# Attention: the first head pair's softmax factors are turned once and read back as rows

## The chip, the core and the metric

The kernel runs on one core of a Trainium2 chip. TensorE multiplies matrices from SBUF into PSUM (eight banks of 128 x 512 float32), VectorE, ScalarE and GpSimd work elementwise, SyncE issues most DMA transfers between DRAM and SBUF. Each engine executes its own instructions in order, and waits at an instruction until what it needs is there. GpSimd works on SBUF alone here: everything that it reads or writes is an SBUF tile. The metric is the device time of one execution in microseconds (us); of the kernel before it is 1876.85 us, the median of three runs (1876.06 to 1878.15).

## The reference, cut to what matters

The program is one decoder layer for 1024 tokens of width 1024 in float32: a half-step feed-forward network, then two token mixers side by side (attention and pooling), merged by gates, then another half-step feed-forward network. Only the attention is touched. It has three groups of four heads of 64 dimensions, each group with its own window and dilation, and the groups' results are combined per head with weights from their softmax denominators:

```python
for g, (window, dilation) in enumerate(DILATED_GROUPS):
    o, lse = dilated_window_attention(q[:, :, hs], k[:, :, hs], v[:, :, hs], window, dilation)
    outs.append(o)
    lses.append(lse)
alpha = jax.nn.softmax(jnp.stack(lses, axis=0), axis=0)
o = jnp.sum(alpha[..., None] * jnp.stack(outs, axis=0), axis=0)
return o.reshape(B, S, ATTN_OUT_WIDTH).astype(v.dtype)
```

So for each token and head there are three factors, one per group. The kernel folds the division by the denominator into them.

## The kernel before, in words

Every float32 product is done as three products of parts (a rounded high part and the low remainder), so most operands exist as a "hi" tile that ScalarE rounds and a "lo" tile that VectorE or GpSimd subtracts.

The attention is one loop over q from 0 to 23. The four heads of a group make two head pairs (hp 0 and 1); a slot s is one block of 128 queries of one head pair and group, for both heads, and there are N = 48 of them, 24 for each pair, in the order of groups 0, 1, 2 for the first pair and 1, 2, 0 for the second. Step q does the work of slots 2q and 2q+1, spread over three steps:

- `scores` (L1948, every second q for two steps ahead): TensorE multiplies queries by keys into PSUM banks with the tag "mm", of which there are four.
- `masked` (L1966, VectorE) adds the mask and keeps the row minimum; `exponents` (L1975, ScalarE) follows and leaves the row sums. Minimum and sum are a slot's statistics.
- one step later `trans_p` (L1995, TensorE) transposes the weights into banks of the tag "acc", four as well; `split_p` makes hi (L2007, ScalarE) and lo (L2010, VectorE).
- two steps later `values` (L2028, TensorE) multiplies by the values into an "acc" bank, and a step after that `gather` (L2051, VectorE) copies the result to the tile `own[hp, g]`: 128 partitions, 64 dimensions of the one head and 64 of the other, by 1024 tokens.

Between these TensorE fills in chunks of four matmuls of the pooling branch (`branch`, L2087, tiles yp), whose banks (also "acc") VectorE empties in `end_branches` (L2101). For ring tiles of the next group, ScalarE and GpSimd split queries and keys (`split_ring`, L1587 and L1588), and in slots 16 to 34 they prepare weights (`first_w_o`, L1823 to L1827).

The statistics of a group go through DRAM to be put in token order (`send_stats`, `get_stats`). From them `make_factors` makes a tile f of 128 tokens x 3 groups x 8 blocks x 2 heads for a head pair. It is a generator that `house` moves on one step at a time: for the first pair at slots 32, 33 and 34, with GpSimd doing most of the arithmetic, and for the second after the loop, with VectorE. It ends by spreading each factor over 64 places (`f_of`), for the first pair on GpSimd (L1913).

`combine(hp, half, ...)` is another generator. For each half of the tokens and each group it turns four blocks of the spread factors with TensorE (`factor_rows`, L1926), which puts them into an "mm" bank with the head dimension along the partitions, as `own` has it; VectorE multiplies `own` by them (L2060), GpSimd adds the groups (L2062), then ScalarE rounds (L2067) and GpSimd subtracts (L2068). For the first pair it is moved on two steps at a time in the odd steps q = 19, 21 and 23 and finished after the loop; there the second pair follows. Both results go into `merge` (L2153) after that.

The order on every engine is the order in which the program calls these functions (`tc.manual_schedule()`). All DMAs named here are issued by SyncE and stand in its order too.

Of the kernel before, what the change touches and what calls it, by code (L numbers as in the profile page):

```python
# [16 lines left out]
P = 128  # L17
# [120 lines left out]
def tile_block(  # L138
# [1748 lines left out]

    f_of = {}

    def make_factors(hp, eng):  # L1890
        st = stats[hp]
        m, l = st[:, :, :, 0:2], st[:, :, :, 2:4]
        top = att_small.tile([P, 1, NT, 2], F32, name=f"top{hp}")
        w = att_small.tile([P, GROUPS, NT, 2], F32, name=f"w{hp}")
        f = att_small.tile([P, GROUPS, NT, 2], F32, name=f"f{hp}")
        every = [P, GROUPS, NT, 2]
        ve.tensor_tensor(top[:, 0], m[:, 0], m[:, 1], op=OP.min)
        ve.tensor_tensor(top[:, 0], top[:, 0], m[:, 2], op=OP.min)
        eng.tensor_tensor(w, top.to_broadcast(every), m, op=OP.subtract)
        yield  # L1900
        ac.activation(w, w, AF.Exp)
        yield
        eng.tensor_tensor(f, w, l, op=OP.mult)
        eng.tensor_tensor(top[:, 0], f[:, 0], f[:, 1], op=OP.add)
        eng.tensor_tensor(top[:, 0], top[:, 0], f[:, 2], op=OP.add)
        ve.reciprocal(top, top)
        eng.tensor_tensor(f, w, top.to_broadcast(every), op=OP.mult)

        f_of[hp] = sums_o.tile([P, GROUPS, NT * 2, HD], F32, tag="f", bufs=1, name=f"f_of{hp}")
        for g in range(GROUPS):  # L1910
            src = f[:, g].rearrange("p i a -> p (i a)")[:, :, None].to_broadcast([P, NT * 2, HD])
            if hp == 0:
                gp.tensor_copy(f_of[hp][:, g], src)  # L1913
            elif g == 1:
                ve.tensor_copy(f_of[hp][:, g], src)
            else:
                ac.activation(f_of[hp][:, g], src, AF.Copy)
        yield
# [136 lines left out]
    def combine(hp, half, adds, lower):  # L2055
# [3 lines left out]
        for g in range(GROUPS):  # L2059
            ve.tensor_tensor(o[g], o[g], factor_rows(hp, g, half), op=OP.mult)  # L2060
            if g > 0:
# [105 lines left out]
    def house(s):  # L2167
# [6 lines left out]
        if u > 0 and i == 4 and slots[s - 5][1] != 0:  # L2174
            get_stats(*slots[s - 5][:2])
        if N // 2 + 8 <= s < N // 2 + 11:
            advance(factors[0])
# [6 lines left out]
    with tc.manual_schedule():  # L2184
# [8 lines left out]
        for q in range(N // 2):  # L2193
            send()
            if q % 2 == 0:
                scores(q)
                scores(q + 1)
            elif N // 4 + 7 <= q:
                advance(combines[0][(q - N // 4 - 7) // 4], 2)
            if q == 0 or q % 2 == 1:  # L2200
# [464 lines left out]
```

## Time and profile before

| | before |
|---|---|
| median of three runs | 1876.85 us |
| profiled execution | 1876.94 us, its span 1874.9 us |
| granted TensorE clock | 0.999 |
| busy: TensorE, VectorE, ScalarE, GpSimd | 99%, 73%, 41%, 42% |
| first pair's transposes of factors (L1926) | from 1098.9 us, 24 of the 48 |
| first pair's GpSimd spreads (L1913) | three, from 1096.1 us |

The span is the time from the first to the last instruction that the profile shows. Busy shares are over the whole span. Matmuls overlap one another, so a busy TensorE need not be at its peak: the distance between the starts of matmuls tells more than their lengths. Names such as L1926 are lines of the program. Of a waiting instruction the profile names the engine whose result came last.

### The profile page before, as it was taken

Reading aid. Unit: us, or ns where it says so; the run is one execution under the profiler, and the core shown is the slowest. Engines: PE = TensorE matmul, PEld = TensorE weight load, DVE = VectorE, ACT = ScalarE, POOL = GpSimd, SP = SyncE. Lnnn points to the kernel's source line nnn. Section 1 sums busy time; section 2 is a strip of 40 time slices with the busy share of each in tenths; the row PEclk is TensorE's granted clock in tenths of the full one; section 3 lists DMA queues with packets and bytes.
Section 4 is the critical chain, followed back from the end, with each engine's and each line's share of the span. In section 5 each row is a group of like instructions: output and inputs, shape, how many; then the busy total and the mean of one; then the engine's idle time right before and its main releaser. Section 6 shows DMA issues by size and latency. Waiting matters only on the chain.

```text
span 1874.9 us, 24458 instructions
## 1 busy us (share of the span) xinstructions
PE 1864.6 (99%) x8690; PEld 1546.4 (82%) x8690; DVE 1369.0 (73%) x1972; ACT 767.7 (41%) x1392; POOL 782.5 (42%) x566
## 2 busy tenths in 40 slices
PE   9999999999999999999999999999999999999998
PEld 7888888888888888888888888888888888888887
DVE  7887866668886776658885896888765566577867
ACT  8322323333345643334445762463333333334344
POOL 4554644452222364445554457544333333313221
PEclk9999999999999999999999999999999999999999
DMA  8134324356565435765678868734342233354654
GB/s 327 45 124 148 122 95 151 123 200 210 189 234 197 158 114 204 253 221 185 213 251 327 309 223 296 266 133 180 119 140 85 90 107 121 127 200 158 224 198 146
DMA packets 147473, 338.10 MB, mean 180 GB/s; under 512 B 17944, under 2 KB 39448, under 8 KB 145816
## 3 DMA queue, kind: packets, MB, share of 16 engines
q1 hardware_dynamic: 143608, 325.70, 50.3%
q10 hardware_dynamic: 3744, 10.85, 1.5%
q8 instruction: 68, 1.11, 0.3%
q14 instruction: 53, 0.43, 0.1%
HBM read 235.90 MB, written 100.60 MB: 179 GB/s over the span
## 4 chain that ended last, share of the span: by engine, by line
PE 54%; DVE 3%; ACT 2%; issue 1%; DMA 1%; POOL 1%; ACTq 0%; SPq 0%; DVEq 0%; POOLq 0%
PE u_mixm L334 15%; PE d_f L904 8%; PE wo L2345 4%; PE yp L2087 1%; PE u_f20a L334 1%; PE u_f21b L334 1%; PE u_f20b L334 1%; PE u_f21a L334 1%; PE u_f210b L334 1%; PE u_f210a L334 1%; PE u_f29b L334 1%; PE u_f29a L334 1%; PE u_f28b L334 1%; PE u_f28a L334 1%; PE u_f27b L334 1%
## 5 line engine op out<-in xcount | busy, mean ns | idle before, releaser
L904 PE MATMUL d_f<-bhi_f,ahi_f 128*128 128x512 f32 x616 | 240.2, 390 | 0.0
L904 PE MATMUL d_f<-bhi_f,alo_f 128*128 128x512 f32 x616 | 239.8, 389 | 0.0
L904 PE MATMUL d_f<-blo_f,ahi_f 128*128 128x512 f32 x616 | 239.6, 389 | 0.0
L861 POOL TENSOR_TENSOR alo_f<-g_f,ahi_f 128x512 fp32r<-128x512 f32 x60 | 89.6, 1511 | 266.2 <-ACT ahi_f L857 266.2
L334 PE MATMUL u_mixm<-xhi_t_mix,wc_mixm 128*128 128x512 f32 x608 | 157.3, 391 | 0.1
L904 PEld LDWEIGHTS d_f<-bhi_f,alo_f 128*128 128x128 f32 x616 | 115.6, 188 | 24.5 <-DVE alo_f L861 0.2
L904 PEld LDWEIGHTS d_f<-bhi_f,ahi_f 128*128 128x128 f32 x616 | 115.7, 188 | 24.2 <-ACT h L424 0.5
L904 PEld LDWEIGHTS d_f<-blo_f,ahi_f 128*128 128x128 f32 x616 | 115.7, 188 | 23.7
L334 PEld LDWEIGHTS u_mixm<-xhi_t_mix,wc_mixm 128*128 128x128 f32 x608 | 113.5, 188 | 23.8 <-ACT wc_mixm L322 0.6
L334 PE MATMUL u_mixm<-xhi_b_mix,wc_mixm 128*128 128x512 f32 x456 | 120.3, 391 | 0.0
L325 POOL TENSOR_TENSOR wc_mixm<-s_mixm,wc_mixm 128x512 fp32r<-128x512 f32 x52 | 77.9, 1499 | 99.1 <-ACT wc_mixm L322 88.2
L334 PEld LDWEIGHTS u_mixm<-xhi_b_mix,wc_mixm 128*128 128x128 f32 x456 | 85.0, 188 | 17.2
L322 ACT ACTIVATE wc_mixm<-s_mixm 128x512 fp32r<-128x512 f32 x76 | 47.0, 628 | 110.4 <-DVE s_mixm L378 54.1
L857 ACT ACTIVATE ahi_f<-g_f 128x1024 fp32r<-128x1024 f32 x84 | 81.9, 975 | 7.9 <-DMA g_f<-gs_f 7.9
L334 PE MATMUL u_mixm<-xlo_t_mix,wc_mixm 128*128 128x512 f32 x304 | 81.3, 389 | 0.0
L325 POOL TENSOR_TENSOR wc_mixm<-raw,wc_mixm 128x512 fp32r<-128x512 f32 x41 | 62.3, 1524 | 38.7 <-ACT wc_mixm L322 35.2
L2345 PE MATMUL wo<-w_o,o_hi 128*128 128x512 f32 x224 | 69.3, 390 | 0.0
L646 POOL TENSOR_TENSOR y_f<-y_f,norm_ffn 128x512 f32<-128x512 f32 x35 | 54.4, 1560 | 35.5 <-DVE y_f L627 25.2
L857 ACT ACTIVATE bhi_f<-s_f2w 128x512 fp32r<-128x512 f32 x55 | 32.9, 628 | 86.2 <-DVE s_f2w L879 67.3
L857 ACT ACTIVATE bhi_f<-s_f1w 128x512 fp32r<-128x512 f32 x55 | 33.1, 629 | 83.8 <-DVE s_f1w L879 71.1
L334 PEld LDWEIGHTS u_mixm<-xlo_t_mix,wc_mixm 128*128 128x128 f32 x304 | 57.1, 188 | 11.9
L861 DVE TENSOR_TENSOR alo_f<-g_f,ahi_f 128x1024 fp32r<-128x1024 f32 (+1 forms) x48 | 59.7, 1245 | 7.6 <-ACT ahi_f L857 7.6
(1357 smaller groups left out, 4822.6 us busy)
## 6 DMA issues: line engine op xcount, KB each, us to landing
g_f<-gs_f SPq DMA_DIRECT2D x70, 512.0 KB
gs_f<-y_f SPq DMA_DIRECT2D x88, 256.0 KB
raw<-in_w2a_dram SPq DMA_DIRECT2D x35, 512.0 KB
raw<-in_w2b_dram SPq DMA_DIRECT2D x35, 512.0 KB
gs_f<-gb_f SPq DMA_DIRECT2D x46, 256.0 KB
raw<-in_w1b_dram SPq DMA_DIRECT2D x22, 512.0 KB
raw<-in_w3b_dram SPq DMA_DIRECT2D x22, 512.0 KB
raw<-in_w1a_dram SPq DMA_DIRECT2D x20, 512.0 KB
```

The lines of the kernel that those rows point to most:

```text
L322: ac.activation(w[:, 0], src, AF.Copy)
L325: eng.tensor_tensor(w[:, 1], src, w[:, 0].bitcast(F32), op=OP.subtract)
L334: pe.matmul(p, a, b, start=(start and n == 0), stop=(n == 11), skip_group_check=not start)
L646: gp.tensor_tensor(c, c, self.sv.norm[:, cols], op=OP.mult)
L857: ac.activation(hi[:, c], src, AF.Copy)
L861: eng.tensor_tensor(lo[:, d], src[:, o], hi[:, d].bitcast(F32), op=OP.subtract)
L904: pe.matmul(self.banks[m][t], l, r, start=(first and q == 0), stop=(last and q == 2))
L2087: pe.matmul(p, a, b, start=(j == 0), stop=(j == 11))
L2345: pe.matmul(banks[m][t], l, r, start=(st == 0 and j == 0 and q == 0), stop=(st == 1 and j == 1 and q == 2))
```

## The change

For the first head pair, the factors are kept by head (3 groups x 2 heads x 8 blocks), TensorE turns them in one transpose of 128 x 48, ScalarE copies the 48 rows to SBUF, and SyncE stores them to DRAM as 48 rows of 128 tokens. Two loads then read them back, one for each head: the rows of the three groups, 1024 tokens each, repeated for 64 partitions. So `f_of[0]` stands as `own` does, and no factors of the first pair are turned into PSUM in `combine`: GpSimd multiplies `own` by them. The generator has five steps for this pair, at the slots 31, 32, 33, 35 and 36, where it had three at 32, 33 and 34. The first pair's combination is moved on by two steps in every q from 20 on (half 0 in 20 and 21, half 1 in 22 and 23). The second pair is done as before, but its tile f too is kept by head, and its spreads read it with another order of the dimensions.

```diff
     f_of = {}
+    f_dram = dram.tile([GROUPS, 2, NT, P], F32, name="f_by_head")
 
     def make_factors(hp, eng):
...
-        f = att_small.tile([P, GROUPS, NT, 2], F32, name=f"f{hp}")
+        by_head = att_small.tile([P, GROUPS, 2, NT], F32, name=f"f{hp}")
+        f = by_head.rearrange("p g a i -> p g i a")
...
         eng.tensor_tensor(f, w, top.to_broadcast(every), op=OP.mult)
 
+        if hp == 0:
+            yield
+            p = bank("mm", "f_turned")[:GROUPS * 2 * NT, :P]
+            pe.transpose(p, by_head.rearrange("p g a i -> p (g a i)"), ident)
+            turned = att_small.tile([GROUPS * 2 * NT, P], F32, name="f_turned")
+            ac.activation(turned, p, AF.Copy)
+            nc.sync.dma_start(f_dram.rearrange("g a i p -> (g a i) p"), turned)
+            yield
         f_of[hp] = sums_o.tile([P, GROUPS, NT * 2, HD], F32, tag="f", bufs=1, name=f"f_of{hp}")
-        for g in range(GROUPS):
-            src = f[:, g].rearrange("p i a -> p (i a)")[:, :, None].to_broadcast([P, NT * 2, HD])
-            if hp == 0:
-                gp.tensor_copy(f_of[hp][:, g], src)
-            elif g == 1:
-                ve.tensor_copy(f_of[hp][:, g], src)
+        if hp == 0:
+            f_of[hp] = f_of[hp].rearrange("p g i d -> p g (i d)")
+            for a in range(2):
+                src = f_dram.rearrange("g a i p -> a g (i p)")[a]
+                nc.sync.dma_start(f_of[hp][a * HD:(a + 1) * HD], src[None].to_broadcast([HD, GROUPS, S]))
+            yield
+        for g in range(GROUPS if hp else 0):
+            src = f[:, g].rearrange("p i a -> p i a")[:, :, :, None].to_broadcast([P, NT, 2, HD])
+            dst = f_of[hp][:, g].rearrange("p (i a) d -> p i a d", a=2)
+            if g == 1:
+                ve.tensor_copy(dst, src)
             else:
-                ac.activation(f_of[hp][:, g], src, AF.Copy)
+                ac.activation(dst, src, AF.Copy)
         yield
...
         for g in range(GROUPS):
-            ve.tensor_tensor(o[g], o[g], factor_rows(hp, g, half), op=OP.mult)
+            if hp == 0:
+                gp.tensor_tensor(o[g], o[g], f_of[hp][:, g, c], op=OP.mult)
+            else:
+                ve.tensor_tensor(o[g], o[g], factor_rows(hp, g, half), op=OP.mult)
...
-        if N // 2 + 8 <= s < N // 2 + 11:
+        if s - N // 2 in (7, 8, 9, 11, 12):
             advance(factors[0])
...
-            elif N // 4 + 7 <= q:
-                advance(combines[0][(q - N // 4 - 7) // 4], 2)
+            if N // 4 + 8 <= q:
+                advance(combines[0][(q - N // 4 - 8) // 2], 2)
```

## The prediction

> **What bounds the kernel now.** I read the page first.
>
> ```profile
> span 1874.9 us, 24458 instructions
> PE 1864.6 (99%) x8690; PEld 1546.4 (82%) x8690; DVE 1369.0 (73%) x1972; ACT 767.7 (41%) x1392; POOL 782.5 (42%) x566
> ```
>
> TensorE is busy 99% of the span, so only what makes TensorE's stream shorter, or makes it wait, counts. The change touches the attention loop between 1086 and 1133 us. There I read the timeline of TensorE, then of ScalarE (columns: start us, length us, engine, line, what, count, and in brackets the idle time before and what ended it).
>
> ```profile
> 1094.26 0.28 PE L2028 MATMUL o<-ehi,v_in 128*128 128x256 f32 x1
> 1096.91 0.66 PE L1995 MATMUL tp<-ident,e 128*128 128x128 f32 x4
> 1099.04 1.04 PE L1926 MATMUL fa<-ident,f_of 128*128 128x128 f32 x8
> 1099.83 0.94 PE L2087 MATMUL yp<-xhi_b_mix,wab 128*128 128x512 f32 x3
> 1113.00 1.09 PE L1995 MATMUL tp<-ident,e 128*128 128x128 f32 x8
> 1121.39 1.04 PE L1995 MATMUL tp<-ident,e 128*128 128x128 f32 x8
> ...
> 1094.56 0.19 ACT L1975 ACTIVATION_READ_ACCUMULATOR e<-e,own_stats 128x1 f32 x1
> 1109.53 0.63 ACT L2067 ACTIVATE att<-o 128x512 fp32r<-128x512 f32 x1 [1.87 <-POOL o L2062]
> 1110.06 0.85 ACT L2007 ACTIVATE ehi<-tp 128x256 fp32r<-128x256 f32 x2
> 1112.68 0.19 ACT L1975 ACTIVATION_READ_ACCUMULATOR e<-e,stats 128x1 f32 x1
> ```
>
> Two things are to be seen. Eight of the transposes to be removed start at 1099.04 and the next matmul starts at 1099.83: they cost 0.79 us, 0.099 us each. And TensorE is only just ahead of ScalarE: the exponents of step q=21 end at 1112.68 + 0.19 = 1112.87, and the transposes that read them (q=22, here called tp21) start at 1113.00. ScalarE works in order, and ahead of these exponents stand the split of q=20 (1110.06) and, at the top of q=21, the copy of the combined heads (L2067, 1109.53), which waits for GpSimd's last add of half 0. So a later GpSimd is a later ScalarE and a later TensorE, with no slack between.
>
> **The change part by part.**
>
> *Removed from TensorE, VectorE and GpSimd.* The first pair has 24 of the transposes on L1926: 24 x 0.099 = 2.4 us of TensorE. One 48-row transpose comes in, costed as the gap of about a transpose, 0.1 to 0.2 us. Were nothing else to happen: **-2.2 us**. VectorE loses six multiplies, GpSimd three spreads (3.02 us) and gains six multiplies. The second pair's spreads read the same 128x1024 elements in another order; I take nothing for that.
>
> ```profile
> L2060 DVE TENSOR_TENSOR o<-o,fa x12: 676/680/687, 1099.7 to 1136.0; 128x512 f32<-128x512 f32 x12
> L2062 POOL TENSOR_TENSOR o<-o,o x6: 1283/1295/1303, 1101.6 to 1136.1; 128x512 f32<-128x512 f32 x6
> 1096.10 3.02 POOL L1913 COPY f_of<-f 128x1024 f32<-128x1024 f32 x3
> 1102.81 2.55 POOL L1588 TENSOR_TENSOR xhi_b_mix<-xhi_b_mix,xlo_b_mix 128x512 fp32r<-128x512 f32 x2
> 1108.20 1.29 POOL L2062 TENSOR_TENSOR o<-o,o 128x512 f32<-128x512 f32 x1 [2.84 <-DVE o L2060]
> ```
>
> A multiply takes 0.68 us on VectorE; on GpSimd the nearest row is its add of the same shape, 1.29 us. Each half of the combination is now five operations in a row on GpSimd before ScalarE may copy (three multiplies, two adds): 5 x 1.28 = **6.4 us**, where GpSimd had two adds. They stand behind the ring's splits of q=19, which end at 1102.81 + 2.55 = 1105.36, so even with the factors there at once the last add ends at 1111.8 instead of 1108.20 + 1.29 = 1109.49: **+2.3 us at least**.
>
> *The factors made one slot earlier* (s=31, 32, 33 instead of 32, 33, 34). The arithmetic on GpSimd now stands between the two halves of other work, and VectorE's reciprocal waits for it.
>
> ```profile
> 1088.33 2.53 POOL L1823 TENSOR_TENSOR w_o_in<-w_o_in,w_o_in 128x512 f32<-128x512 f32 x2
> 1091.98 2.55 POOL L1827 TENSOR_TENSOR w_o<-w_o_in,w_o 128x512 fp32r<-128x512 f32 x2 [0.52 <-ACT w_o L1826]
> 1094.49 0.30 POOL L1903 TENSOR_TENSOR f<-w,stats 128x48 f32<-128x48 f32 x1
> 1095.16 0.22 POOL L1905 TENSOR_TENSOR top<-top,f 128x16 f32<-128x16 f32 x1
> 1091.29 0.62 ACT L1826 ACTIVATE w_o<-w_o_in 128x512 fp32r<-128x512 f32 x1
> 1089.88 0.69 DVE L2010 TENSOR_TENSOR elo<-tp,ehi 128x512 fp32r<-128x512 f32 x1 [0.23 <-ACT ehi L2007]
> 1091.25 1.28 DVE L2051 COPY o<-o 64x256 f32<-64x256 f32 x2
> 1095.42 0.25 DVE L1906 RECIPROCAL top<-top 128x16 f32<-128x16 f32 x1 [0.73 <-POOL top L1905]
> ```
>
> Now the reciprocal stands in q=17 and waits 0.73 us. Moved to the end of q=16, VectorE reaches it after the split that ends at 1089.88 + 0.69 = 1090.57. GpSimd's order there is: the adds of w_o (two halves from 1088.33, the first step of the factors between them, to about 1091.2), then the first half of L1827, which waits for ScalarE's copy (1091.29, now behind the small exponential: done about 1092.1) and takes 1.27, to 1093.4, and only then L1903 to L1905, which now take 1095.38 - 1094.49 = 0.89 us: 1094.3. **VectorE stands still for 3.7 us**; behind it are the gather of q=17 (now at 1091.25, then at about 1094.45: 3.2 later) and the masks of q=17. TensorE: PSUM's four "acc" banks hold at that time a finished and a begun branch, the transposed weights and the output awaiting that gather, so the values matmul of 1094.26 needs the bank that the gather frees. It frees it at 1091.25 + 1.28 = 1092.53 now, 1.73 us ahead; 3.2 late makes TensorE wait 1.5 us. The stats read that the first step needs must also be there four microseconds earlier; no wait for it shows today, and I take none. Bounds for this whole edit on TensorE: 0 to 3.2 us, taken 1.5. The turned factors hold one of the scores' four banks until ScalarE has copied them (1098.25 below); that can cost the scores of q=18 and 19 part of a microsecond, inside the same bounds.
>
> *Turned factors to DRAM and back.* ScalarE's copy of the turned factors stands behind the exponents of q=17, which end at 1094.75 now and 3.2 later then: 1097.95; with the copy 1098.25. Then SyncE: the store, and behind it the by_pool store, the values' loads, the stats read, and then two loads of 64 partitions x 3 x 4 KB, 1.57 MB together. They also wait for the store to land: 2.97 us after issue in the chain's row of another store.
>
> ```profile
> 1094.72 0.32 SPq L2111 DMA_DIRECT2D by_pool<-gb  x1
> 1095.08 1.26 SPq L1608 DMA_DIRECT2D v_in<-v  x2
> 1096.45 0.39 SPq L1886 DMA_DIRECT2D stats<-st  x1
> 1135.47 2.97 DMA by_pool<-gb
> v_in<-v SPq DMA_DIRECT2D x6, 512.0 KB
> 1094.50:1095.50 1.00, 1.00 (x11) 0.87 (x9) 0.27 (x2) 0.25 (x2) 0.73 (x4) 1.00 0.00 0
> 1095.50:1105.00 9.50, 9.50 (x92) 8.58 (x93) 8.77 (x28) 6.35 (x22) 9.19 (x9) 1.00 0.93 280
> 1099.50:1100.00 0.50, 0.50 (x7) 0.50 (x6) 0.34 (x2) 0.50 (x5) 0.50 (x1) 1.00 1.02 410
> 665.00:670.00 5.00, 5.00 (x26) 4.05 (x25) 3.79 (x6) 2.80 (x5) 2.97 (x3) 1.00 0.26 83
> ```
>
> (The last four rows: stretch, its length, busy time of five engines, granted clock, DMA share, GB/s.) The by_pool store's data runs 0.8 us after its issue (nothing moves before 1095.5). With the factor store ahead of it, it is issued at 1098.6 and runs from 1099.4. In front of the factors stand three blocks of 512 KB, 1.57 MB, and the factors are as much again. At 280 GB/s, the mean of the stretch in which the same queue works now, each 1.57 MB takes 5.6 us and the factors are there at 1110.6; at 410, its best half microsecond, 3.84 each and 1107.1. Between the two: **1109**. The slow end is the last row, table loads to 64 partitions from repeated DRAM rows: 83 GB/s, which would be 19 us. But there the DMA share is 0.26, a quarter of the engines at 320 GB/s per full share, and that source repeats 4 rows where this one repeats 64; I take the loop's rate.
>
> [...]
>
> *The sum.* Factors at 1109, five GpSimd operations: the last add of half 0 ends at 1115.4 (1113.5 to 1117.0) against 1109.49: **5.9 us late** (4.0 to 7.5). Behind it on ScalarE are the copy, the split of q=20 and the exponents, 1113.00 - 1109.53 = 3.47 us, and tp21 is 5.9 late. VectorE's split of q=20 is late as well, behind ScalarE's. From tp21 to tp23 is 1121.39 - 1113.00 = 8.39 us now. TensorE loses 12 transposes there (1.2 us) but can't use it: from the last add of half 0 come ScalarE's copy (0.63), GpSimd's lower part (1.28) and its next five operations (6.4), 8.3 us, and then the same stretch of copy, split and exponents as before tp21 (3.47): 11.8 us to tp23, where it is 1121.39 - 1109.49 = 11.9 now. So the 2.4 us saved on TensorE go into these waits. The TensorE wait of 1.5 us at q=17 is already in the 5.9, since it only makes the chain start later. After tp23 the work is the same, but VectorE has three multiplies less, and three short waits could go (who waited <- for whom, us in all, times, longest):
>
> ```profile
> PEld ya L2153 <- DVE att L2068: 0.3, 1, 0.3
> PEld ya L2153 <- DVE o L2060: 0.3, 1, 0.3
> PEld wo L2345 <- DVE o_lo L2333: 0.5, 1, 0.5
> ```
>
> Up to 1.1 us; I take 0.4. Net **+5.5 us**, with ends +1.2 (2.3 less 1.1) and +7.5. The profiled execution took 1876.94 us, 2.04 over its span, and lies 0.09 above the median of 1876.85, so: **1882.4 us**, 0.3% slower.
>
> **The rivals.**
>
> *GpSimd is bound by its own work alone* (no stall of VectorE, or a load that arrives by 1105): then only the +2.3, less 0.4 to 1.1 in the tail: 1878.1 to 1878.8. For it: the queue stands idle at 1094.5 to 1095.5, so an early store would get through at once. Against: the 3.7 us follow from the order of the instructions. 14%.
>
> *Faster*: GpSimd's five operations end by 1109.5, ScalarE doesn't wait longer than now, and TensorE's shorter stream shows: 1876.94 - 2.2 = 1874.7. It decides from a load that is there by 1103.1 and ring splits that end by then; against it stand 1105.36 for the splits and the ScalarE end of 1112.87 against 1113.00, which leaves no room for TensorE to get ahead. 6%.
>
> *TensorE's clock falls in the wait*. At tp21 the wait comes in one piece: 5.9 late, less the 1.5 of q=17, less what the removed transposes would have gained by then (1.2), so 4 to 5 us with nothing for TensorE to do. All stretches above show a granted clock of 1.00, and no wait in them is that long. If the clock were halved for as long as such a wait, 4 us, the work in it would take 2 us more: 1884.4; if it lasted until tp23, 4.2 more: 1886.6. [...] 12%.
>
> *The loads of 64 partitions run at half the loop's rate*: 1.57 MB at 140 GB/s, 5.6 us more, 1888; at the rate midway, 2.8 more, 1885.2, which I take for it. For it: nothing in the trace but the slow table loads. 12%. At the table loads' own 83 GB/s it is some 13 us more, 1896: 2%.
>
> *The change does not do what it says*: the transposes were hidden and the new waits are too, 1876.9. The 0.79 us between 1099.04 and 1099.83 speak against it. 2%.
>
> **How the numbers follow.** Forecast 52%, and the rivals 14, 6, 12, 12, 2 and 2. About 0.2%, 3.75 us, is what a measurement of this kernel can tell from no change. Under +3.75 lie the GpSimd-only case, the case without effect and about 10 of the forecast's 52: same 26%; faster 6%; slower 42 + 12 + 12 + 2 = 68%. The forecast's own range is 1878.1 to 1884.4. The range takes in half of the first rival, the clock and the half rate: 1877.5 to 1887.5.
>
> **What would show it.** In the changed profile: VectorE's reciprocal waiting 3 to 4 us for GpSimd near 1091; a values matmul (L2028) or tp17 1 to 2 us later than today; GpSimd's first multiply waiting for a DMA until 1107 to 1111; ScalarE's copy L2067 waiting some 6 us or more for GpSimd; TensorE's longest wait in tp21, for the exponents; no wait of GpSimd on VectorE left in the loop. I am wrong if the first multiply starts before 1106, if tp21 comes before 1116, or if a clock under 0.95 shows after it.

## The result and the profile after

The changed kernel takes 1888.26 us, the median of four runs (1888.08 to 1889.82), beside 1877.23 us of the kernel before in the same comparison: 1.0062 times as long, with a 95% interval of 1.0050 to 1.0074. It is 11.0 us slower. The forecast was 1882.4, slower by 5.5 us, with a range of 1877.5 to 1887.5: the sign is right, the size is half of what came, and the time lies 0.8 us above the range.

The page of the changed kernel's profile (its execution took 1888.15 us, 11.2 more than the one shown of before):

```profile
span 1886.2 us, 24413 instructions
PE 1865.0 (99%) x8667; PEld 1544.6 (82%) x8667; DVE 1366.0 (72%) x1966; ACT 768.3 (41%) x1393; POOL 785.1 (42%) x569
```

TensorE's share is 99% as before, so this view doesn't tell where the 11 us went. The attention loop's timeline does (start, length, engine, line, what, count, and in brackets the idle time before and what ended it). Lines have moved: L1995 is L2010 now, L2028 is L2043, L2062 is L2080, L2067 is L2085 and L2153 is L2171.

```profile
1094.39 0.25 DVE L1908 RECIPROCAL top<-top 128x16 f32<-128x16 f32 x1 [3.18 <-POOL top L1907]
...
1095.88 0.36 PE L2043 MATMUL o<-ehi,v_in 128*128 128x256 f32 x1 [1.72 <-DVE o L2066]
...
1097.99 0.33 SPq L1917 DMA_DIRECT2D f_by_head<-f_turned  x1
...
1101.99 1.28 SPq L1924 DMA_DIRECT2D f_of<-f_by_head  x2
...
1114.83 2.48 POOL L2076 TENSOR_TENSOR o<-o,f_of 128x512 f32<-128x512 f32 x2 [7.91 <-DMA f_of<-f_by_head]
...
1119.95 1.26 POOL L2080 TENSOR_TENSOR o<-o,o 128x512 f32<-128x512 f32 x1
...
1121.24 0.63 ACT L2085 ACTIVATE att<-o 128x512 fp32r<-128x512 f32 x1 [11.88 <-POOL o L2080]
...
1123.17 2.15 PE L2010 MATMUL tp<-ident,e 128*128 128x128 f32 x8 [8.79 <-ACT e L1990]
...
1132.12 1.64 PE L2010 MATMUL tp<-ident,e 128*128 128x128 f32 x8
...
1144.57 1.63 PE L2171 MATMUL ya<-att,ya 128*128 128x512 f32 x6
```

In the kernel before, the first `ya` matmul stood at 1133.24:

```profile
1133.24 4.03 PE L2153 MATMUL ya<-att,ya 128*128 128x512 f32 x15
```

From top to bottom this is the forecast's chain: VectorE waits 3.18 us for GpSimd, TensorE 1.72 us for VectorE, the store is issued at 1097.99, the loads at 1101.99. Then the size goes wrong: GpSimd's first multiply starts at 1114.83, where 1109 was forecast. The last add of half 0 keeps that distance to the forecast (1115.4). It ends at 1119.95 + 1.26 = 1121.21, 11.7 us later than before; the transposes for q=22 (tp21) start 10.2 later, those for q=24 (tp23) 10.7, and the first `ya` matmul, at 1144.57 instead of 1133.24, 11.3. The whole spans differ by 11.3 as well, so all of the loss has arisen by the time of that add, and what stands ahead of it is GpSimd's wait of 7.91 us for the factors.

The same stretch in windows of 2 us (the window, its length, then busy time of TensorE, weight load, VectorE, ScalarE and GpSimd; granted clock; DMA share; GB/s):

```profile
1100.00:1102.00 2.00, 2.00 (x13) 1.59 (x11) 1.79 (x5) 2.00 (x8) 1.21 (x1) 1.00 0.58 179
...
1104.00:1106.00 2.00, 2.00 (x29) 1.86 (x29) 1.67 (x3) 2.00 (x9) 1.61 (x2) 1.00 1.18 326
1106.00:1108.00 2.00, 2.00 (x19) 1.69 (x16) 1.74 (x10) 1.36 (x6) 0.92 (x1) 1.00 1.03 199
...
1110.00:1112.00 2.00, 2.00 (x12) 1.66 (x11) 1.61 (x9) 0.00 (x0) 0.00 (x0) 1.00 1.03 205
...
1114.00:1116.00 2.00, 0.38 (x8) 0.17 (x4) 0.00 (x0) 0.00 (x0) 1.17 (x1) 1.00 1.05 390
1116.00:1118.00 2.00, 0.00 (x0) 0.00 (x0) 0.00 (x0) 0.00 (x0) 1.92 (x3) 0.67 1.02 388
1118.00:1120.00 2.00, 0.00 (x0) 0.00 (x0) 0.00 (x0) 0.00 (x0) 1.92 (x3) 0.50 1.10 360
```

While the factors are loaded (1106 to 1114) all sixteen DMA engines are busy (a share of 1.00 to 1.06), but they move 199 to 221 GB/s; the transfers behind them move 360 to 390 at a share of 1.02 to 1.10. And the clock goes down to 0.50 after TensorE has stood still for 2.3 us. There are two suspects, then: the loads' rate and the clock. A third reading would be that the five GpSimd operations or the earlier slot are worth more than forecast.

### The profile page after: what moved, and what is told of

It is laid out like the page before. It is cut to its first block, busy times and chain, and to the rows that moved or that the text cites. A ratio compares the mean times of both kernels' runs of the same rounds, so it can differ in the third digit from the quotient of the medians.

```text
span 1886.2 us, 24413 instructions
## 1 busy us (share of the span) xinstructions
PE 1865.0 (99%) x8667; PEld 1544.6 (82%) x8667; DVE 1366.0 (72%) x1966; ACT 768.3 (41%) x1393; POOL 785.1 (42%) x569
## 3 DMA queue, kind: packets, MB, share of 16 engines
q8 instruction: 68, 1.11, 0.3%
## 4 chain that ended last, share of the span: by engine, by line
PE 91%; DVE 3%; ACT 2%; DMA 2%; issue 1%; POOL 1%; SPq 0%; ACTq 0%; POOLq 0%
PE d_f L904 21%; PE u_mixm L334 19%; PE wo L2363 4%; PE ya L2171 1%; PE yp L2105 1%; PE u_f20a L334 1%; PE u_f21b L334 1%; PE u_f20b L334 1%; PE u_f21a L334 1%; PE u_f210b L334 1%; PE u_f210a L334 1%; PE u_f29b L334 1%; PE u_f29a L334 1%; PE u_f28b L334 1%; PE u_f28a L334 1%; PE u_f27b L334 1%
```

## The experiments

Each kernel was compared with the kernel before on the same chip, whose median was 1876.83 to 1877.14 us there. All edits are to the changed kernel unless said otherwise.

### Other rows, loaded early

```diff
         eng.tensor_tensor(f, w, top.to_broadcast(every), op=OP.mult)
...
+            for a in range(2):
+                src = gate_dram[a][0:GROUPS, 0]
+                nc.sync.dma_start(f_of[hp][a * HD:(a + 1) * HD], src[None].to_broadcast([HD, GROUPS, S]))
...
-            for a in range(2):
-                src = f_dram.rearrange("g a i p -> a g (i p)")[a]
-                nc.sync.dma_start(f_of[hp][a * HD:(a + 1) * HD], src[None].to_broadcast([HD, GROUPS, S]))
```

> The two loads of the factor rows are taken from the gate's stored rows (64 partitions x 3 x 4 KB, as before, but not the factors, so the output is not the reference's) and issued right after the third step of the factors, some 10 us earlier; the turning and the store stay. Theory (load late by 5.8 us, of which GpSimd would have needed part anyway): GpSimd's first multiply starts when the ring's splits end, near 1107, the five operations end near 1113.3, the eight transposes for q=22 start near 1117 instead of 1123.2, the granted clock stays at 1.00, and the time is 8 us less than the changed kernel's: about 1880. Rival A (the loads are all of the loss): 1875 to 1877. Rival B (the chain of five GpSimd operations and the earlier slot are the loss, not the load): within 2 us of the changed kernel, 1886 to 1888.

Measured: 1881.56 us, 1.0024 times before (1.0015 to 1.0032), so +4.4 instead of +11.0. GpSimd's first multiply starts at 1107.82, when its ring splits are done, and the clock stays at 1.00. The loads now run alone, with no other transfer beside them (windows of this run):

```profile
1094.00:1096.00 2.00, 1.15 (x6) 0.60 (x4) 0.66 (x2) 0.00 (x0) 1.48 (x6) 1.00 1.03 215
1096.00:1098.00 2.00, 1.18 (x10) 1.18 (x10) 1.96 (x11) 0.90 (x5) 1.19 (x1) 1.00 1.06 203
```

They still move 203 to 215 GB/s: the low rate isn't a fight with the values' loads. The loads' lateness is worth 6.6 us; 4.4 us are something else. So both rivals fall, and the theory's 8 us were a little too many.

### Early rows, and the factors' steps in their old slots

```diff
-        if s - N // 2 in (7, 8, 9, 11, 12):
+        if s - N // 2 in (8, 9, 10, 11, 12):
```

With the early rows:

> Both at once: other rows loaded early (so the output is not the reference's) and the first three steps of the factors in the slots that they had before the change. Theory (with the load out of the way the earlier slot's stall shows, 1.5 us as forecast, and what is left is GpSimd's five operations, +2.3 less what the tail wins): 1.5 us less than with early loads alone: 1879 to 1880.5. Rival A (the slot costs nothing on the path, GpSimd's operations are all of the 4.4 us): 1881 to 1882. Rival B (the slots were all of it): 1877 to 1878.

Measured: 1879.32 us (1.0014, 1.0005 to 1.0023), +2.5 on its chip where early rows alone had +4.4: the earlier slot costs 1.9 us here. The reciprocal waits 0.75 us, and what is left is +2.5, for which the forecast had +2.3 (five operations on GpSimd instead of two). With the loads as in the changed kernel:

> The factors' first three steps go back to the slots that they had before the change (s=32, 33, 34); the turning and the loads stay at s=35 and s=36. Theory (the earlier slot costs some 1.5 us, because VectorE's reciprocal stands still for GpSimd and TensorE for VectorE, and everything behind it, the store of the factors too, moves with it): the reciprocal waits under 1 us, the values matmul near 1094 doesn't wait, the store leaves 1 to 1.5 us earlier, the first multiply starts 1 to 1.5 us earlier, and the time is 1 to 2 us less than the changed kernel's: 1886 to 1887. Rival A (TensorE only waits elsewhere, for the turning of factors that are now made in the slot ahead of it): the time stays at 1888. Rival B (the earlier slot pays by an earlier store): slower than the changed kernel, 1889 or more.

Measured: 1888.10 us (1.0058, 1.0046 to 1.0071), no difference that can be told from the changed kernel's 1.0062. The store leaves 1.2 us earlier (1096.80), but the first multiply comes at 1114.30, 17.5 us after it instead of 16.8. The stall is real, but in the changed kernel the factors come at nearly the same time with or without it.

### What holds the loads: where they go, or what they read

One load of the same bytes in the same 4 KB pieces, to 128 partitions:

```diff
-            for a in range(2):
-                src = f_dram.rearrange("g a i p -> a g (i p)")[a]
-                nc.sync.dma_start(f_of[hp][a * HD:(a + 1) * HD], src[None].to_broadcast([HD, GROUPS, S]))
+            src = f_dram[:, 0].rearrange("g i p -> g (i p)")
+            nc.sync.dma_start(f_of[hp], src[None].to_broadcast([P, GROUPS, S]))
```

> One load of the same 1.57 MB in the same pieces of 4 KB to all 128 partitions at the same place, all of them from the first head's rows (so the output is not the reference's). Theory (a load that goes to 64 neighbouring partitions is held at half the rate by where it goes): 350 GB/s or more behind the values' loads, the factors there 3.5 to 4 us earlier after the store than the changed kernel's 16.8 us, the time 1884 to 1885. Rival (the pieces or the many reads of the same rows hold the rate): 200 to 220 GB/s, 16 to 17 us after the store, 1888.

And 64 partitions as before, but from 64 different stretches of memory:

```diff
             for a in range(2):
-                src = f_dram.rearrange("g a i p -> a g (i p)")[a]
-                nc.sync.dma_start(f_of[hp][a * HD:(a + 1) * HD], src[None].to_broadcast([HD, GROUPS, S]))
+                src = gate_dram[a].rearrange("(d x) b c -> d (x b) c", x=2)[:, :GROUPS]
+                nc.sync.dma_start(f_of[hp][a * HD:(a + 1) * HD], src)
```

> Two loads of 64 partitions x 3 x 4 KB at the same place, from 64 different stretches of stored rows and not from repeated ones (so the output is not the reference's). Theory (the 64 partitions make the half rate): 200 to 220 GB/s from about 1106 to 1114, the first multiply near 1114.8, 1888. Rival (the repeated rows make it): 350 GB/s or more, the first multiply near 1110 or 1111, 1883 to 1885.

With 128 partitions, two windows and then a line of the timeline:

```profile
1106.00:1108.00 2.00, 2.00 (x18) 1.70 (x15) 1.73 (x10) 1.35 (x7) 0.95 (x1) 1.00 1.06 360
...
1110.00:1112.00 2.00, 2.00 (x12) 1.66 (x10) 1.67 (x9) 0.00 (x0) 0.14 (x1) 1.00 1.02 380
```

```profile
1111.86 2.53 POOL L2075 TENSOR_TENSOR o<-o,f_of 128x512 f32<-128x512 f32 x2 [4.91 <-DMA f_of<-f_by_head]
```

The rate is 286 to 380 GB/s, the first multiply starts 13.8 us after the store's issue (1098.03) instead of 16.8, and the time is 1884.85 (one run): +8.0 on its chip, where the changed kernel had +11.0. With 64 partitions and different rows the windows show 192 to 227 GB/s until 1112, the first multiply comes at 1116.22 and the time is 1889.93 (one run). So it is the 64 partitions, not the repeated rows, that hold the rate near 210 GB/s here. By what means they do isn't shown.

### The true factors over 128 partitions

Three loads, one for each group, both heads in one:

```diff
+            for g in range(GROUPS):
+                src = f_dram[g].rearrange("a i p -> a (i p)")[:, None].to_broadcast([2, HD, S])
+                nc.sync.dma_start(f_of[hp][:, g], src)
```

> The same bytes by three loads, one for each group over all 128 partitions, in place of two loads of 64 partitions. Theory (loads of 64 partitions move at half the rate because of their partitions): the stretch behind the stats read shows 350 GB/s or more, the last factors are there near 1110 instead of 1114.8, GpSimd's first multiply starts earlier still since it needs only the first group, and the time is 4 to 6 us under the changed kernel's: 1882 to 1884. Rival (the rate is low because 64 descriptors read the same row, or because the rows come from a small piece of memory): 200 to 220 GB/s as before, the last factors at 1114 or 1115; only the first multiplies come earlier, 1885 to 1888.

Measured: 1909.3 us (1.0170, 1.0156 to 1.0184), the worst of all, and neither the theory's time nor the rival's. The windows say why:

```profile
1110.00:1112.00 2.00, 2.00 (x12) 1.70 (x11) 1.84 (x9) 0.00 (x0) 0.00 (x0) 1.00 0.13 53
```

A DMA share of 0.13 is that of two busy engines among sixteen, at 26 GB/s each. The source has two blocks (one for each head), as many as there are busy engines. That the one sets the other is an inference, not shown by this run alone. With it in mind the factors were next repeated eight times by GpSimd, turned in three transposes, stored, and read back as 16 blocks of 8 partitions for each group:

```diff
+            for g in range(GROUPS):
+                src = f_dram[g].rearrange("(x i) p -> x (i p)", i=NT)[:, None].to_broadcast([16, 8, S])
+                nc.sync.dma_start(f_of[hp][:, g], src)
```

> The changed kernel with the true factors loaded so that a load covers all 128 partitions: the factors are repeated eight times before they are turned (three turnings of 128 rows), stored as 16 blocks of rows for each group, and read back by three loads in which each block serves 8 partitions. Theory (the half rate of the 64-partition loads made the factors 3 us late, the rest of the lateness is the blocks ahead of them in the queue): 300 GB/s or more behind the values' loads, the first multiply 12 to 14 us after the store's issue instead of 16.8, and since it needs only the first group perhaps 1 to 2 us earlier still; GpSimd's three copies cost about 1 us ahead of it; the time 1884 to 1886. Rival (16 blocks use the engines no better, or the store of eight times the bytes takes the gain): 1887 or more.

Measured: 1885.48 us (1.0043, 1.0031 to 1.0056), the theory's time. The DMA share is 1.03 to 1.09 from 1106 to 1114, that of all sixteen engines, as inferred, though the rate is only 238 to 267 GB/s. The first multiply starts at 1110.02, 12.0 us after the store, since it needs the first group alone.

### Both halves from two queues, and the loads ahead of the others

```diff
-                nc.sync.dma_start(f_of[hp][a * HD:(a + 1) * HD], src[None].to_broadcast([HD, GROUPS, S]))
+                (nc.sync, nc.scalar)[a].dma_start(f_of[hp][a * HD:(a + 1) * HD], src[None].to_broadcast([HD, GROUPS, S]))
```

> The second head's load (partitions 64 to 127) is issued from ScalarE's queue at the same slot, so that both halves of the partitions are written at once; bytes and rows are as in the changed kernel. Theory (a load to one half of the partitions runs at half the rate, and both halves together at the full): 300 GB/s or more from 1104 to 1110 instead of 200 to 220, the last factors there near 1110 (three other blocks of 512 KB go through the first queue), GpSimd's first multiply 4 to 5 us earlier, and the time 4 to 6 us less than the changed kernel's: 1882 to 1884. Rival A (the source's repeated rows or the size of the descriptors set the rate): 200 to 220 GB/s all the same, factors at 1113 or later, 1886 to 1889. Rival B (a load on ScalarE's queue delays ScalarE's exponents by its issue): the first multiply is early and the time falls by less than half of it.

Measured: 1888.44 us (1.0058, 1.0044 to 1.0072). One window of 2 us in the view of the DMA queues (q1 is SyncE's, q10 ScalarE's; packets, MB, share of 16 engines):

```profile
DMA packets 134, 0.54 MB, mean 271 GB/s; under 512 B 1, under 2 KB 1, under 8 KB 134
q1 hardware_dynamic: 68, 0.27, 49.8%
q10 hardware_dynamic: 66, 0.27, 48.6%
```

This is 1108 to 1110. With both halves under way the rate is 271 to 293 GB/s, better than 199 to 221; but ScalarE's load, issued at 1102.41, moved nothing before 1106.5, and the first multiply came 16.3 us after the store instead of 16.8. The time is rival A's, but its reason, the low rate all the same, doesn't hold. With the first head's load issued right behind the store, ahead of `by_pool` and the values, and the second head's from ScalarE a slot later:

> The first head's load is issued right behind the store of the factors on SyncE, ahead of the by_pool store and the values' loads, and the second head's from ScalarE's queue one slot later. Theory (with the factors there in time only the five operations of GpSimd and the earlier slot are left, which the run with other data put at 4.4 us): factors there before 1107, the first multiply when the ring's splits are done, clock 1.00, and the time is that of the run with early loads, 1881 to 1882. Rival (SyncE's wait for the store to land delays the values' loads and the by_pool store, and these are needed): the transposes or the values of q=19 to 21 wait for v_in, 1884 or more. Second rival (the loads compete with the values' loads and stay the last to arrive): the first multiply at 1109 or later, 1883 to 1885.

Measured: 1886.80 us (1.0054, 1.0041 to 1.0066); the first multiply comes 15.6 us after the store. Again ScalarE's load (issued at 1101.21) moves nothing before 1107. That is the second rival, a little slower still; the first doesn't hold, since no wait for the values shows. Why the second queue starts so late wasn't settled.

### The clock

The score matmuls of q=22 and q=23 are repeated into the same banks, with the same result, so that TensorE has work in the wait:

```diff
-                scores(q)
-                scores(q + 1)
+                scores(q, 6 if q == 22 else 1)
+                scores(q + 1, 6 if q == 22 else 1)
```

> The score matmuls of q=22 and q=23 are done six times over into the same banks with the same result, so that TensorE has some 7 us more of matmuls in the wait before the transposes for q=22 and idles under 3 us there. Theory (the clock falls because TensorE idles for 9 us, and the slower clock costs about 2 us after it): the granted clock stays at 1.00 from 1114 to 1128, the transposes for q=22 start where they start now (1123.2), and the time is 1.5 to 2.5 us less: about 1886. Rival (the clock's fall lies beside waits for ScalarE and GpSimd and costs nothing): the clock stays up and the time is the changed kernel's, 1888. Below these: if the extra matmuls themselves delay the masks of q=22, the time is more than 1888.

Measured: 1889.33 us (1.0061, 1.0048 to 1.0075). Inconclusive: the matmuls ended at 1121.5, the factors came 1.2 us later than in the changed kernel, and in the remaining 3 us the clock fell to 0.50 again. So seven times over:

> The repeats of the score matmuls once more, seven times over instead of six, so that they end near 1123 and TensorE idles for less than 1.5 us before the transposes for q=22 (with six, 2.5 us without a matmul were enough for a clock of 0.5 for 3.4 us). Theory (the slower clock costs about 2 us after the wait): the granted clock stays at 1.00 from 1114 to 1130, and if the factors land as in the changed kernel, the time is 1886 to 1886.5; counted from the transposes for q=22 to the first ya matmul it takes 1.5 to 2 us less than the changed kernel's 21.4. Rival (the slower clock is hidden beside ScalarE's and GpSimd's work): the clock stays at 1.00 and the stretch from the transposes for q=22 to the first ya matmul stays at 21.4 us, the time at 1888 to 1889.

Measured: 1888.93 us (1.0063, 1.0051 to 1.0076). One window of this run:

```profile
1124.00:1126.00 2.00, 1.87 (x12) 1.12 (x11) 1.96 (x5) 1.95 (x8) 2.00 (x3) 1.00 0.02 8
```

and in its timeline:

```profile
1124.00 1.77 PE L2010 MATMUL tp<-ident,e 128*128 128x128 f32 x7
...
1145.39 1.85 PE L2171 MATMUL ya<-att,ya 128*128 128x512 f32 x7
```

The clock is 1.00 throughout, and from tp21 to the first `ya` it is 1145.39 - 1124.00 = 21.39 us; in the changed kernel, with half the clock for its first 3.8 us, 1144.57 - 1123.17 = 21.40. The rival holds: the fall of the clock costs nothing here. The likely reason is that TensorE isn't what the stretch waits for: ScalarE's exponents end one every 0.49 us, and behind them the next ones wait for GpSimd's next five operations.

### What the removal is worth

In all runs of this section the factors' first three steps are back in their old slots. In the first two VectorE multiplies the first pair again, from SBUF, in the slots of the kernel before, with other rows loaded early. First with the loads at the third step of the factors:

```diff
-                gp.tensor_tensor(o[g], o[g], f_of[hp][:, g, c], op=OP.mult)
+                ve.tensor_tensor(o[g], o[g], f_of[hp][:, g, c], op=OP.mult)
...
-            if N // 4 + 8 <= q:
-                advance(combines[0][(q - N // 4 - 8) // 2], 2)
+            elif N // 4 + 7 <= q:
+                advance(combines[0][(q - N // 4 - 7) // 4], 2)
```

> The same, and the first pair's six multiplies are back on VectorE, from SBUF, in the slots of the kernel before. So only this is left of the change: no spreading on GpSimd, no transposes of the factors but the one, and loads that nobody waits for (other rows, so the output is not the reference's). Theory (24 transposes of 0.099 us are worth 2.2 us if nothing takes their place, but ScalarE is only 0.13 us behind TensorE and holds part of it): 1875 to 1876.5, below the kernel before. Rival A (ScalarE holds all of it): 1876.5 to 1877.5, no difference from before. Rival B (the multiplies read SBUF at another speed, or the loads and the turning cost by themselves): over 1878.

Measured: 1880.13 us (1.0018, 1.0009 to 1.0027), but VectorE waited 2.93 us for the rows, so it says nothing of the removal. Then with the loads at the first step, 7.5 us earlier (1082.5 instead of 1090.0):

> VectorE multiplies the first pair from SBUF in the slots of before, with other rows loaded some 6 us earlier than in the last such run (so the output is not the reference's), so that VectorE doesn't wait for them: only the transposes are gone. Theory (24 transposes of 0.099 us, 2.2 us net, of which ScalarE and VectorE let part through): no wait of VectorE for f_of, 1875 to 1876.8. Rival A (the end of the loop is set by VectorE's second factors, so the gain is given back there): 1876.5 to 1877.5. Rival B (VectorE's multiplies from SBUF take longer than 0.68 us, because both operands are in SBUF while GpSimd works): multiplies over 1 us, 1878 or more.

Measured: 1879.65 us (1.0013, 1.0004 to 1.0022). VectorE no longer waits for rows, and yet (a line of the timeline, and the row of the tile's view with its shortest, median and longest in ns):

```profile
1100.68 2.89 DVE L2079 TENSOR_TENSOR o<-o,f_of 128x512 f32<-128x512 f32 x2
```

```profile
L2079 DVE TENSOR_TENSOR o<-o,f_of x6: 682/686/1768, 1100.7 to 1124.5; 128x512 f32<-128x512 f32 x6
```

Two multiplies beside GpSimd's ring splits take 2.89 us, where two take 1.28 otherwise, and the two splits take 2.98 instead of 2.53. That is rival B.

The other way is to keep GpSimd's multiplies and the true factors, but to let nothing in the loop wait for them: the halves are combined at q=22 and q=23, and ScalarE's copies stand behind the loop.

```diff
-            if N // 4 + 8 <= q:
-                advance(combines[0][(q - N // 4 - 8) // 2], 2)
+            if q >= 22:
+                advance(combines[0][q - 22], 3)
...
         advance(factors[1])
-        advance(combines[0][1])
+        advance(combines[0][0])
         trans_p(q - 1)
```

> The true factors, loaded as in the changed kernel, GpSimd multiplies as there; but the two halves are combined at q=22 and q=23, and ScalarE's copies of them stand behind the loop; the factors' steps are in the slots of before. Theory (the whole loss is that the loop's ScalarE waits for GpSimd, and that for the load; nothing before the merges needs the first pair's heads): no wait of ScalarE for L2080 in the loop, clock 1.00, the transposes for q=22 near 1113, the time 1875 to 1877. Rival A (the work moves into the stretch behind the loop, where ScalarE and GpSimd hold the second pair's factors and combination): 1878 to 1881. Rival B (something else in the loop waits for the loads, such as the loads of ya or by_pool behind them in the queue): 1882 or more.

Measured: 1880.72 us (1.0020, 1.0011 to 1.0028), rival A's time. But for 0.62 us ahead of the turning, TensorE has no wait in the loop: tp21 isn't late and the clock is 1.00. TensorE reaches the end of the loop early, and there waits 2.18 us. VectorE's arithmetic for the second pair's factors, in the kernel before:

```profile
1121.84 0.17 DVE L1897 TENSOR_TENSOR top<-stats 128x16 f32<-128x16 f32 x1
1122.04 0.17 DVE L1898 TENSOR_TENSOR top<-top,stats 128x16 f32<-128x16 f32 x1
...
1124.59 0.18 DVE L1904 TENSOR_TENSOR top<-f 128x16 f32<-128x16 f32 x1
...
1125.30 0.21 DVE L1907 TENSOR_TENSOR f<-w,top 128x48 f32<-128x48 f32 x1
1125.61 0.69 DVE L1915 COPY f_of<-f 128x1024 f32<-128x1024 f32 x1
```

and with the later combination, GpSimd being at its multiplies and adds all the while:

```profile
1120.31 1.15 DVE L1899 TENSOR_TENSOR top<-stats 128x16 f32<-128x16 f32 x1
...
1121.83 0.89 DVE L1900 TENSOR_TENSOR top<-top,stats 128x16 f32<-128x16 f32 x1 [0.37 <-DMA stats<-st]
...
1124.35 1.11 DVE L1906 TENSOR_TENSOR top<-f 128x16 f32<-128x16 f32 x1
...
1126.00 0.91 DVE L1909 TENSOR_TENSOR f<-w,top 128x48 f32<-128x48 f32 x1
...
1127.00 1.58 DVE L1930 COPY f_of<-f 128x1024 f32<-128x1024 f32 x1
...
1128.10 0.66 PE L1941 MATMUL fa<-ident,f_of 128*128 128x128 f32 x4 [2.18 <-ACT f_of L1932]
```

The same five instructions take 5.64 us instead of 1.42. To tell GpSimd's work from other causes, its five operations on half 1 (three multiplies, two adds) were left out:

> The later combination again, but GpSimd's five operations on the second half of the first pair are left out (the half is passed on as it is, so the output is not the reference's). Theory (with the later combination the loop was free of waits, and 4 us were lost where VectorE's short instructions with two operands in SBUF stood behind GpSimd's multiplies: 1.15, 0.89, 1.11, 0.91 and 1.58 us instead of 0.17 to 0.25 and 0.69): these instructions are back at 0.17 to 0.25 and 0.69, TensorE's wait of 2.18 us at the first fa goes down to under 0.5, and the time is 2.5 to 4 us less than the later combination's 1880.7: 1877 to 1878. Rival A (VectorE was held by late stats or its own work): the short instructions stay long, 1880 to 1881. Rival B (they get short but the end of the loop waits for something else, ScalarE's copies of f_of or the second pair's adds): short instructions, 1879.5 or more.

Measured: 1877.64 us, 1.0004 times before (0.9995 to 1.0012), no difference; but this kernel leaves out work that the result needs. In this run GpSimd is idle from about 1124 on:

```profile
1125.52 0.17 DVE L1906 TENSOR_TENSOR top<-f 128x16 f32<-128x16 f32 x1
...
1126.22 0.25 DVE L1909 TENSOR_TENSOR f<-w,top 128x48 f32<-128x48 f32 x1
1126.56 0.69 DVE L1930 COPY f_of<-f 128x1024 f32<-128x1024 f32 x1
...
1127.62 0.66 PE L1941 MATMUL fa<-ident,f_of 128*128 128x128 f32 x4 [0.62 <-ACT f_of L1932]
```

The theory holds: it was GpSimd, though TensorE's wait is 0.62 us where under 0.5 was expected. The ends of the instructions fit it. With the later combination GpSimd's rows are

```profile
1120.15 2.52 POOL L2076 TENSOR_TENSOR o<-o,f_of 128x512 f32<-128x512 f32 x2
...
1124.08 1.35 POOL L2076 TENSOR_TENSOR o<-o,f_of 128x512 f32<-128x512 f32 x1
```

and end at 1122.67 and 1125.43; VectorE's instructions of 0.89 and 1.11 us end at 1122.72 and 1125.46, 0.05 and 0.03 us behind them. What the two engines share isn't shown. The changed kernel has such a place too, which the prediction didn't count. In their earlier slot VectorE's first instructions for the factors run beside GpSimd's ring splits:

```profile
1085.56 2.53 POOL L1588 TENSOR_TENSOR qk_in<-qk_in,qk_hi 128x512 fp32r<-128x512 f32 x2 [1.38 <-ACT qk_hi L1587]
...
1086.92 1.20 DVE L1900 TENSOR_TENSOR top<-top,stats 128x16 f32<-128x16 f32 x1
```

The split ends at 1088.09 and VectorE's instruction, which took 0.17 us before, at 1088.12.

Last, all remedies at once: loads as 16 blocks right behind the store, the old slots, GpSimd's ten operations in q=20 and 21, copies behind the loop.

> All remedies at once: loads over 128 partitions as above, issued right behind the store and ahead of the by_pool store and the values' loads; the factors' steps in the slots of before; GpSimd's ten operations in q=20 and q=21, ScalarE's copies of the heads behind the loop. Theory (the factors come by 1107, GpSimd is done by 1120.5, before VectorE's short instructions for the second pair's factors, so that these take 0.17 to 0.25 us again): no wait in the loop over 0.7 us, the second pair's first transposes (fa) at 1126.5 to 1127, the time 1876 to 1877.5, so at most as much below the kernel before as a measurement can tell. Rival A (SyncE's wait for the store delays the values' loads): waits for v_in, 1878 to 1882. Rival B (GpSimd is done later than 1122 and VectorE's short instructions are held): 1879 to 1881 as with the later combination.

Measured: 1879.54 us (1.0012, 1.0003 to 1.0021), +2.5 on its chip instead of the changed kernel's +11.0, but still slower than before. VectorE's short instructions are at 0.17 to 0.29 us, but two new waits stand in the profile:

```profile
1097.03 0.80 PE L1920 MATMUL f_turned<-ident,f_of 128*128 128x128 f32 x3 [1.00 <-POOL f_of L1915]
...
1124.44 0.17 DVE L1900 TENSOR_TENSOR top<-top,stats 128x16 f32<-128x16 f32 x1 [2.22 <-DMA stats<-st]
```

TensorE waits 1.00 us for the factors that it is to turn, and the second pair's stats come 2.2 us late: their load is issued at 1119.92 into a queue that is busy from 1104 to 1132 (a DMA share of 0.94 or more), with the transfers that were put back ahead of it. None of the versions tried is faster than the kernel before.

## Why the prediction was right in sign and wrong in size

*What bounds the kernel* held. ScalarE's place just behind TensorE carried the delay of GpSimd to TensorE: it is 11.7 us at the add, 10.2 at the first transposes of tp21, which now start as soon as the first exponents end, and 11.1 at the matmul behind the last of them (1124.98 instead of 1113.85). The wait of ScalarE for L2080, 11.88 us, is the longest of the loop.

*Five operations instead of two, +2.3 at least*: right. GpSimd's five end 6.4 us after the first starts (1114.83 to 1121.21), as forecast, and with load and slots out of the way 2.5 us were left.

*The earlier slot*: right in its waits (3.18 us of VectorE and 1.72 of TensorE, forecast 3.7 and 1.5) and worth 1.9 us when nothing covers it. In the changed kernel the loads cover most of it.

*Factors there at 1109*: the term that failed. They were there at 1114.8, 5.8 us later and past the slow end of the prediction's own bounds for them (1110.6). The step behind the error is the choice "I take the loop's rate": the loop's rate was that of transfers over all 128 partitions. The trace of before had just one row with 64 partitions, and it was set aside for its few busy engines (0.26) by scaling it to 320 GB/s at a full share. That was a sound reason against its 83 GB/s, but at a full share the loads to 64 partitions moved 199 to 221, neither 320 nor the 280 to 410 of the sum.

How the 5.8 us divide can be estimated by adding up the bytes of windows of 0.5 us, with the queue taken as strictly in order. The blocks in front were then through at about 1105.3, where the sum has 1104.1; from 1100.5 to 1101.5 the queue moved only 41 to 43 GB/s, and why isn't known. The factors' own bytes took from there to about 1112.7, which is 7.4 us where the sum has 4.7 (midway between 5.6 and 3.84). And some 2 us then passed until the multiply, for which the sum had no term. The same count for the load to 128 partitions gives 4.9 us for the bytes and again 2.1 behind them. So by this estimate about 2.7 us are the rate of the loads, 2 the way from the last bytes to the multiply, and 1.2 the blocks in front. Of these, the rate is shown by a run of its own: with the same bytes to 128 partitions the first multiply came 3.0 us earlier after the store.

The rival "half the loop's rate", which had 12%, hit the time of 1888 by luck: it priced the loads at 140 GB/s, which no run shows (they moved 199 to 221), and had nothing for the other two parts.

*No recovery after the add*: right in the main; 11.7 us late at the add, 11.3 at `ya`. The tail won nothing: from tp23 to `ya` it takes 12.45 us instead of 11.85, where 0.4 less was taken.

*The clock rival* had its event, not its price. The clock fell to 0.50 in a wait of 8.8 us, which the prediction's own list has as a sign of being wrong; but the 2 to 4.2 us that the rival took for it are shown by no run: from tp21 to `ya` it is 21.40 us with the fall and 21.39 in the run with TensorE kept busy. The first multiply before 1106 and tp21 before 1116 didn't come.

*The faster rival* would have needed factors at 1103.1. Even with rows that nobody waited for, no version became faster. What stood in place of the 2.2 us of transposes was seen: a wait of TensorE at the turning (0.62 to 1.00 us, where the prediction costed 0.1 to 0.2 for the turning), VectorE's instructions held beside GpSimd's (five that take 5.64 us instead of 1.42), and the second pair's factors at the end of the loop. How much each of these costs stays open, and so does whether the transposes were worth 2.2 us, since no run has their removal alone.

## What to carry to other kernels

A transfer's price was set here by where it goes as much as by its bytes: the same 1.57 MB moved at 199 to 221 GB/s to 64 partitions, at 286 to 380 to 128, and at 51 to 53 to 128 from a source of two blocks. So before costing a load at the rate of its neighbours, compare partitions and the number of blocks in its outer dimension with theirs, and if they differ, let the range reach to half the rate. Moving elementwise work to an engine with idle time was not free here: ScalarE waited in order behind it (11.88 us at L2080), and beside GpSimd's work VectorE's instructions of 0.17 us took up to 1.20; look for both. And a low clock in a profile is a symptom until a run with the clock kept up is faster: 0.50 for 3.8 us after tp21's start cost nothing here.

## What the runs showed of the hardware that was not expected

- A load that repeats two blocks of DRAM rows over 128 partitions ran at a DMA share of 0.12 to 0.13, that of two of the sixteen engines: 51 to 53 GB/s, and 1909 us. One of 16 blocks ran at a share of 1.03 to 1.09, at 238 to 267 GB/s.
- A load to 64 partitions ran at 203 to 215 GB/s with nothing beside it, and at 199 to 221 among others. Two such loads to both halves from two queues ran at 271 to 293 GB/s together, but the second queue's first packets came at least 4.1 and 5.8 us after its issue (1102.41 and 1106.5; 1101.21 and 1107.0).
- VectorE's instructions of 128x16 elements, 0.17 us alone, took up to 1.20 us beside GpSimd, and a multiply of 128x512 from SBUF up to 1.77 instead of 0.68. GpSimd lost less in return: two splits of 2.53 us took 2.98.
- The clock fell about 2.3 us after the last matmul in the changed kernel (1114.4, 1116.7), 2.6 in the first run with repeated scores, and about 4 us with two queues. It came back 3.8 us after matmuls began again in the changed kernel (1123.17, 1126.9), about 3 in the first run with repeated scores (1124.4, 1127.5) and about 6 with two queues (1123.69, 1129.7).
